# A hybrid decoder block on one core: 16x16 blocks gathered on chip, one solve for two mixers, sums of norms moved, no adds on POOL

## The chip, the core and the metric

The kernel runs on one core of a Trainium2 chip, and the metric is the device time of one execution in microseconds, as the median of several. A core has a matrix engine (TensorE, PE in the profile; PEld are its weight loads), a vector engine (VectorE, DVE), a scalar engine (ScalarE, ACT), a general one (GpSimd, POOL) and a fifth that here only issues transfers (SyncE, SP). Each engine runs its own queue in order. Sixteen DMA engines move data between DRAM and on-chip memory; a transfer is issued from the queue of SP, ACT or POOL.

## What is computed

One layer (`DEPTH = 1`) over 256 tokens of width 2048, in fp32:

```python
h = rms_norm(x, norm_mix_pre)
p = h @ w_in                                    # all mixers' inputs and gates
y_a = rglru_branch(...)                         # conv4, gated linear recurrence
y_b = gated_deltanet_branch(...)                # 8 heads of 128, chunks of 64
y_c = rwkv7_branch(...)                         # 16 heads of 64
m = sum_b sigmoid(gate_b) * (y_b @ w_branch[b])
x = x + rms_norm(m @ w_out, norm_mix_post)
h = rms_norm(x, norm_ffn_pre)
x = x + rms_norm((silu(h @ w_gate) * (h @ w_up)) @ w_down, norm_ffn_post)
```

Of the delta-rule mixer y_b the kernel needs, per head and chunk, the inverse of a unit lower triangular matrix:

```python
m = where(strict, beta[..., None] * (k @ k.T) * decay, 0)
sol = triangular_solve(m + eye(64), rhs, lower=True, unit_diagonal=True)
```

The RWKV mixer y_c is written as a recurrence over tokens in the reference; the kernel runs it by chunks of 64 and needs inverses of the same kind.

## The kernel before

**The products.** Every large product is done in three: activations and weights are each split in a high and a low part (`xh`, `xl`, `wh`, `wl`). `weights` (L190 on) loads 1 MB of weights into a tile `raw` from SP's queue (L203), ACT casts half of it into `wh` (L214), DVE subtracts to get `wl` (L216). There are three buffers each of `raw`, `wh` and `wl`. One `wh`/`wl` pair feeds 24 products of 256 columns (`block_b`, L241 to L243, the projections into the mixers) or 12 of 512 columns (`block_a`, L262 to L264, the rest).

**The mixers** run in four quarters `q` (two DeltaNet heads, four RWKV heads, a quarter of the LRU's channels). `rwkv_quarter` and `gdn_pair` are generators: each runs up to the `yield` in `inverse64`, then `lru_quarter` is written out, then the two are resumed, RWKV first. A scheduler lays each engine's queue out before the run, by the order in the program, dependences and its own estimate of durations; `high_priority` pulls an instruction ahead and `issue_after` sets a lower bound. So the mixers' small steps stand among the products of the next projections in PE's queue.

**The inverse** (`inverse64`, L370). A 64x64 triangle is inverted from its 16x16 diagonal blocks upwards. Lane p of DVE shall hold one row of each inverse and needs a whole block for it. RWKV has eight 64x64 matrices per lane half (`nu = 8`, out of `st`), DeltaNet four (`nu = 4`, out of `U`). Eight small DMAs from POOL's queue write a mixer's blocks to a DRAM tile `dblk` (L381), and one more reads it back into `B`, every block spread to 16 lanes (L383): 1 MB for RWKV, 512 KB for DeltaNet. Behind the `yield` come a copy of 16 unit columns (L388) and 15 steps of a product and a subtraction (L392, L393), for each mixer alone, held back behind `last`, the LRU's last instruction. Then merges to 32x32 and 64x64 follow, with transposes on DVE (L406, L417) and small products on PE.

**Norms and the end.** `product_a` (L1082) forms m @ w_out, and later the last product w_down, in four column blocks j and two halves t of 128 tokens. For each, ACT sums squares (L1090) and DVE multiplies with the norm's weight (L1091). After the last block the four sums are added (L1105, L1167), DVE and POOL form the reciprocal root (L296, L297), and the residual is added: L1110 behind w_out, whose result is then split for the next products (L308 to L313), and behind w_down, for each half, three blocks in one DVE instruction each (L1173), the fourth as a scaling on ACT (L1175) and an add on POOL (L1176). L1177 writes the output.

Of the kernel before, what the change touches and what calls it, by code (L numbers as in the profile page):

```python
# [8 lines left out]
F32 = mybir.dt.float32  # L9
F32R = mybir.dt.float32r  # L10
AF = mybir.ActivationFunctionType
# [129 lines left out]
class Builder:  # L141
# [227 lines left out]
    def inverse64(self, nu, diag16, block, transposed):  # L369
# [3 lines left out]
        nc, mp, n = self.nc, self.mp, nu * 32  # L373


        dd = self.dp.tile([8, nu, 16, 16], F32, name=self.uid("dblk"))
        for r in range(8):
            src = diag16(r)
            dst = dd[r].rearrange("(u n) j t -> j u n t", n=src.shape[2]) if len(src.shape) == 4 else \
                dd[r].rearrange("u j t -> j u t")  # L380
            nc.gpsimd.dma_start(dst, src)  # L381
        B = (self.u8 if nu == 8 else self.u4)("B").rearrange("p (u j t) -> p u j t", u=nu, j=16)
        nc.gpsimd.dma_start(B.rearrange("p u j t -> p (u j t)"),  # L383
                            dd.rearrange("r u j t -> r (u j t)").unsqueeze(1).to_broadcast([8, 16, nu * 256]))
        after = yield
        xc = mp.tile([P, nu, 16], F32, name=self.uid("xc"), tag=f"xc{nu}", bufs=1)
        with self.tc.issue_after(after):
            nc.vector.tensor_copy(xc, self.cst("d16", 0, 16).unsqueeze(1).to_broadcast([P, nu, 16]))  # L388
        for j in range(15):
            m = 15 - j  # L390
            t = mp.tile([P, nu, 16], F32, name=self.uid("xt"), tag=f"xt{nu}", bufs=2)
            nc.vector.tensor_tensor(t[:, :, 0:m], B[:, :, j, j + 1:16], xc[:, :, j:j + 1].to_broadcast([P, nu, m]), ALU.mult)  # L392
            nc.vector.tensor_tensor(xc[:, :, j + 1:16], xc[:, :, j + 1:16], t[:, :, 0:m], ALU.subtract)  # L393
# [63 lines left out]
    def rwkv_quarter(self, q, kS, rS, vS, up, y):  # L457
# [110 lines left out]
        X, = yield from self.inverse64(8, lambda r: st8[16 * r:16 * r + 16, :, (r < 4)::2, 16 * r:16 * r + 16],  # L568
# [128 lines left out]
    def gdn_pair(self, q_, qS, kS, vS, sz, y):  # L697
# [70 lines left out]
        J, JT = yield from self.inverse64(4, lambda r: h4(U)[16 * r:16 * r + 16, :, 16 * r:16 * r + 16],  # L768
# [61 lines left out]
    def lru_quarter(self, q, xS, gg, lru, y):  # L830
# [36 lines left out]
        last = nc.vector.tensor_tensor(h, h, gg, ALU.mult).ins  # L867
        nc.sync.dma_start(y[:, q * 512:(q + 1) * 512], h)
        return last


def build(tc, aps, out):
# [117 lines left out]
    def lru(q):  # L990
        s = direct(BLK_LX + q, 3)
        g = kept(BLK_LG + q, AF.Gelu_apprx_tanh)
        b.tmp_tag = "tl"
        return b.lru_quarter(q, s, b.get(g, "gg"), aps["lru"], y[0])

    for q in range(4):
        s = [direct(o + q, 1) for o in (BLK_RK, BLK_R, BLK_RV)]
        b.tmp_tag = "tr"
        rwkv = b.rwkv_quarter(q, *s, aps["up"], y[2])
# [4 lines left out]
        gdn = b.gdn_pair(q, *s, b.get(z, "z"), y[1])  # L1004
        next(gdn)
        last = lru(q)
        for tag, part in (("tr", rwkv), ("tg", gdn)):
            b.tmp_tag = tag
            with contextlib.suppress(StopIteration):
                part.send(last)  # L1010
# [71 lines left out]
    def product_a(w, ah, al, kts, hm, nw, ssq):  # L1082
        for j in range(4):
# [14 lines left out]
    product_a(aps["w_out"], mh, ml, KD, hm, n2, ssq)  # L1098
    x1d = [b.dp.tile([P, D], F32, name=f"x1d{t}") for t in range(2)]
    xh, xl = acts("h")  # L1100
    with tc.high_priority(FIRST):
        tots = [fp.tile([P, 6], F32, name=f"tot{t}") for t in range(2)]
        r1 = []
        for t in range(2):
            nc.vector.tensor_reduce(tots[t][:, 0:1], ssq[:, t], AX.X, ALU.add)  # L1105
            r1.append(b.rstd(fp, tots[t][:, 0:1], 1, 1.0 / D, EPS))
# [93 lines left out]
```

## Time and profile before

| | us |
|---|---|
| median of 3 runs | 1867.28 |
| their range | 1865.79 to 1868.06 |
| the profiled execution | 1864.51 |
| its span, first to last instruction | 1862.7 |
| PE busy | 1831.9 |
| DVE busy | 1113.6 |
| ACT busy | 850.6 |
| POOL busy | 82.5 |

The profile has one execution. Its times count from the first instruction; a group's line gives what it wrote and read (out<-in), its shape, how often it occurs, its busy time and the mean of one. The four mixer quarters lie between about 50 and 880 us, the branches and w_out up to 1111 us, the feed-forward part after that.

### The profile page before, as it was taken

What the parts mean: (1) busy time and instruction counts of PE and PEld (TensorE: products, weight loads), DVE (VectorE), ACT (ScalarE), POOL (GpSimd) and SP (SyncE); (2) the same over time, 40 slices, a digit from 0 to 9 for tenths busy, and PEclk for the clock granted to TensorE, in tenths of its full rate; (3) what the DMA queues carried; (4) which work ended last, traced back from release to release, by engine and by line L of the source; (5) the groups of instructions that cost most, each with busy time, mean ns of one, the idle gap of its engine ahead of it and who ended that gap; (6) DMA issues with size and microseconds to landing.
All of it is one profiled execution on the core that took longest, in us unless ns stands there. A gap on an engine that the chain in (4) does not pass through costs nothing.

```text
span 1862.7 us, 27857 instructions
## 1 busy us (share of the span) xinstructions
PE 1831.9 (98%) x11516; PEld 1582.6 (85%) x11516; DVE 1113.6 (60%) x1622; ACT 850.6 (46%) x1055; POOL 82.5 (4%) x150
## 2 busy tenths in 40 slices
PE   9999999999999999999999999999999999999997
PEld 9999997989898988778788878888888888888886
DVE  6768667766776576746665556554554445544444
ACT  7445345434543464444444446444444444443442
POOL 0011001200120002000000000000000000000000
PEclk9999999999999999999999999999999999999998
DMA  7565445653556345846865556555555555655553
GB/s 262 179 185 195 157 137 189 169 183 133 183 167 194 131 163 190 244 164 248 296 219 182 197 186 246 183 193 191 185 198 183 185 199 182 216 191 199 187 201 113
DMA packets 62799, 354.15 MB, mean 190 GB/s; under 512 B 9168, under 2 KB 10960, under 8 KB 23632
## 3 DMA queue, kind: packets, MB, share of 16 engines
q1 hardware_dynamic: 50832, 328.23, 50.9%
q10 hardware_dynamic: 7328, 15.36, 2.3%
q0 software_dynamic: 4512, 8.79, 1.9%
q8 instruction: 90, 1.47, 0.3%
q14 instruction: 37, 0.30, 0.0%
HBM read 337.27 MB, written 15.07 MB: 189 GB/s over the span
## 4 chain that ended last, share of the span: by engine, by line
PE 53%; issue 38%; DMA 3%; DVE 3%; ACT 1%; POOL 0%; ACTq 0%; DVEq 0%; SPq 0%; POOLq 0%
PE mm L264 8%; PE mm L263 8%; PE mm L262 8%; PE mm L242 7%; PE mm L243 7%; PE mm L241 7%; DMA raw<-in_w_in_dram 2%; DVE wl L216 1%; DMA raw<-in_w_mix_dram 1%; PE px L562 1%; PE pr L585 1%; PE pr L596 0%; ACT wh L214 0%; PE psa L592 0%; PE px L746 0%
## 5 line engine op out<-in xcount | busy, mean ns | idle before, releaser
L216 DVE TENSOR_TENSOR wl<-raw,wh 128x1024 fp32r<-128x1024 f32 x590 | 720.7, 1223 | 611.8 <-ACT wh L214 609.6
L214 ACT CAST wh<-raw 128x1024 fp32r<-128x1024 f32 x590 | 620.0, 1052 | 855.3 <-PE mm L264 592.3
L241 PE MATMUL mm<-xh,wh 128*128 128x256 f32 x1200 | 343.3, 286 | 5.0 <-ACT wh L214 5.0
L243 PE MATMUL mm<-xh,wl 128*128 128x256 f32 x1200 | 344.0, 287 | 2.5 <-DVE wl L216 1.5
L242 PE MATMUL mm<-xl,wh 128*128 128x256 f32 x1200 | 344.1, 287 | 1.6 <-DVE xl L909 1.5
L263 PE MATMUL mm<-wl,hh 128*128 128x512 f32 x704 | 274.7, 390 | 0.0
L264 PE MATMUL mm<-wh,hl 128*128 128x512 f32 x704 | 274.6, 390 | 0.0
L262 PE MATMUL mm<-wh,hh 128*128 128x512 f32 x704 | 251.0, 392 | 2.0 <-DVE rstd L296 1.5
L241 PEld LDWEIGHTS mm<-xh,wh 128*128 128x128 f32 x1200 | 231.1, 193 | 7.1 <-ACT wh L214 5.8
L243 PEld LDWEIGHTS mm<-xh,wl 128*128 128x128 f32 x1200 | 231.0, 193 | 4.2 <-DVE wl L216 1.9
L242 PEld LDWEIGHTS mm<-xl,wh 128*128 128x128 f32 x1200 | 231.1, 193 | 3.1 <-DVE xl L909 2.2
L262 PEld LDWEIGHTS mm<-wh,hh 128*128 128x128 f32 x704 | 132.4, 188 | 29.4 <-ACT hh L311 2.5
L263 PEld LDWEIGHTS mm<-wl,hh 128*128 128x128 f32 x704 | 132.6, 188 | 27.6 <-DVE wl L216 0.4
L264 PEld LDWEIGHTS mm<-wh,hl 128*128 128x128 f32 x704 | 132.5, 188 | 27.6
L263 PE MATMUL mm<-wl,xh 128*128 128x512 f32 x384 | 151.1, 394 | 0.9 <-DVE wl L216 0.9
L264 PE MATMUL mm<-wh,xl 128*128 128x512 f32 x384 | 150.5, 392 | 0.0
L262 PE MATMUL mm<-wh,xh 128*128 128x512 f32 x384 | 141.7, 393 | 0.5 <-ACT wh L214 0.5
L264 PE MATMUL mm<-wh,al 128*128 128x512 f32 x352 | 136.9, 389 | 0.0
L263 PE MATMUL mm<-wl,ah 128*128 128x512 f32 x352 | 136.9, 389 | 0.0
L262 PE MATMUL mm<-wh,ah 128*128 128x512 f32 x352 | 123.6, 389 | 0.0
L297 POOL TENSOR_TENSOR rstd<-rstd,mhalf 128x8 f32<-128x8 f32 (+3 forms) x23 | 29.7, 1296 | 1439.1 <-DVE rstd L296 1439.1
L263 PEld LDWEIGHTS mm<-wl,xh 128*128 128x128 f32 x384 | 72.1, 188 | 17.3 <-DVE wl L216 1.9
(294 smaller groups left out, 2009.0 us busy)
## 6 DMA issues: line engine op xcount, KB each, us to landing
raw<-in_w_in_dram SPq DMA_DIRECT2D x72, 1024.0 KB, 4.9
raw<-in_w_mix_dram SPq DMA_DIRECT2D x48, 1024.0 KB, 5.0
raw<-in_w_gate_dram SPq DMA_DIRECT2D x44, 1024.0 KB, 4.9
raw<-in_w_up_dram SPq DMA_DIRECT2D x44, 1024.0 KB, 4.9
raw<-in_w_down_dram SPq DMA_DIRECT2D x44, 1024.0 KB, 4.9
raw<-in_w_branch_dram SPq DMA_DIRECT2D x24, 1024.0 KB, 5.0
raw<-in_w_out_dram SPq DMA_DIRECT2D x16, 1024.0 KB, 4.8
keep<-stage ACTq DMA_DIRECT2D x28, 256.0 KB, 5.2
```

What stands on the lines that cost most here:

```text
L214: nc.scalar.copy(wh[:, :n], s)
L216: nc.vector.tensor_tensor(wl[:, :n], s, wh[:, :n].bitcast(F32), ALU.subtract)
L241: nc.tensor.matmul(o, hs, xh[:, k], start=(k == 0 and c == 0), stop=False, skip_group_check=True)
L242: nc.tensor.matmul(o, hs, xl[:, k], start=False, stop=False, skip_group_check=True)
L243: nc.tensor.matmul(o, ls, xh[:, k], start=False, stop=(k == kts - 1), skip_group_check=True)
L262: nc.tensor.matmul(ps[t], xh[:, k, ts], h, start=(k == 0), stop=False)
L263: nc.tensor.matmul(ps[t], xh[:, k, ts], l, start=False, stop=False)
L264: return nc.tensor.matmul(ps[t], xl[:, k, ts], h, start=False, stop=(k == kts - 1))
L297: nc.gpsimd.tensor_tensor(r, r, self.mhalf.to_broadcast([P, n]), ALU.pow)
L562: nc.tensor.matmul(ps[h][:, n * P:(n + 1) * P], bkc[hs, c, n], arc[hs, c, n], start=True, stop=True)
L585: nc.tensor.matmul(pq[bb, us], st[u][:, n, bb], sav[:, n, us], start=not n, stop=True, skip_group_check=True)
```

## The change

1. The 16x16 blocks no longer go through DRAM. `inverse64` copies them on chip into a tile `C` of 16 columns per matrix: for each group of 32 lanes, ACT writes one 16-column half times a 0/1 column (L398), DVE adds the other half times its 0/1 column (L396). Two blocks then lie under each other in 32 lanes.
2. A new `solve16` does the 15 steps for both mixers at once (12 matrices side by side). In step j a `stream_shuffle` on DVE (L378) spreads row j of both blocks over their 16 lanes each, into one of three row buffers; product (L379) and subtraction (L380) follow. `C`, the result and the three buffers share one tile `sv`, allocated ahead of `st` from the same pair of large buffers that `st` and `B` used.
3. The solve is written ahead of `lru_quarter`, and nothing holds it behind `last` any more.
4. In `product_a` the sums' addition and the reciprocal root of half t are written as soon as its last squares are summed, ahead of that half's last product with the norm's weight, for both norms.
5. At the end two of four blocks are scaled on ACT and added by DVE; POOL adds nothing.

```diff
-    def inverse64(self, nu, diag16, block, transposed):
...
-            nc.gpsimd.dma_start(dst, src)
...
-        after = yield
...
+    def solve16(self, C, xc, rows):
+        nc = self.nc
+        nu = C.shape[1]
+        nc.vector.tensor_copy(xc, self.cst("d16", 0, 16).unsqueeze(1).to_broadcast([P, nu, 16]))
         for j in range(15):
             m = 15 - j
...
+            t = rows[j % 3][:, :, 0:m]
+            nc.vector.stream_shuffle(t, C[:, :, j + 1:16], [j] * 16 + [16 + j] * 16)
+            nc.vector.tensor_tensor(t, t, xc[:, :, j:j + 1].to_broadcast([P, nu, m]), ALU.mult)
+            nc.vector.tensor_tensor(xc[:, :, j + 1:16], xc[:, :, j + 1:16], t, ALU.subtract)
+
+    def inverse64(self, C, diag, block, transposed):
...
+        for i in range(4):
+            for h in range(2):
+                s = diag(i, h)
+                c = C[32 * i:32 * i + 32]
+                c = c.rearrange("p (u n) t -> p u n t", n=s.shape[2]) if len(s.shape) == 4 else c
+                half = self.cst("blk16", 16 * h, 1)[32 * i:32 * i + 32]
+                if h:
+                    nc.vector.scalar_tensor_tensor(c, s, half, c, ALU.mult, ALU.add)
+                else:
+                    nc.scalar.activation(c, s, AF.Copy, scale=half)
+        xc = yield
...
+        sv = b.u8("sv")[:, 0:5 * 192].rearrange("p (i u t) -> p i u t", i=5, t=16)
+        C, xc = sv[:, 0], sv[:, 1]
...
-        last = lru(q)
...
+        b.solve16(C, xc, [sv[:, i] for i in range(2, 5)])
+        lru(q)
...
                     nc.scalar.activation(junk, ps[t], AF.Square, accum_out=ssq[:, t, j:j + 1])
+                    if j == 3:
+                        rms(t)
                     nc.vector.tensor_tensor(hm[:, t, js], ps[t], nw[:, js], ALU.mult)
...
+        for j in (3, 2):
+            nc.scalar.activation(o[j], o[j], AF.Identity, scale=r4[t])
+        for j in (0, 1, 3, 2):
+            if j < 2:
+                nc.vector.scalar_tensor_tensor(o[j], o[j], r4[t], x[j], ALU.mult, ALU.add)
             else:
-                nc.scalar.activation(od[:, t, js], od[:, t, js], AF.Identity, scale=r4[t])
-                nc.gpsimd.tensor_tensor(od[:, t, js], od[:, t, js], x1[t][:, js], ALU.add)
...
+                nc.vector.tensor_tensor(o[j], o[j], x[j], ALU.add)
```

How the queues stand. First POOL's, before, from the small DMAs of quarter 1 on (`slab` are the projections' outputs, whose margins POOL clears; `sav` is an RWKV tile):

```order
L542 MEMSET sav_2689 64x2x256 x2
L381 DMA dblk_3330<-U_3303 16x4x16 x8
L381 DMA dblk_2737<-st_2712 16x8x16 x8
L383 DMA B_3339<-dblk_3330 128x1x1024
L383 DMA B_2746<-dblk_2737 128x1x2048
L297 TENSOR_TENSOR rstd_4096<-rstd_4096,mhalf 128x4
```

Now the same place on POOL:

```order
L297 TENSOR_TENSOR rstd_2608<-rstd_2608,mhalf 128x8
L548 MEMSET sav_2637 64x2x256 x2
L297 TENSOR_TENSOR rstd_3990<-rstd_3990,mhalf 128x4
L336 MEMSET slab_688_5419 128x2x3
L336 MEMSET slab_902_6873 128x2x3
```

The eighteen DMAs between the clearing of `sav` and the next root are gone from the queue.

DVE in quarter 1, before, from the LRU's last product `h` on (`xc` is the solve's result, `xt` its product, `wl` a weight cast):

```order
L867 TENSOR_TENSOR h_3619<-h_3619,gg_3583 128x512
L388 COPY xc_3623<-cst_t 128x128
L388 COPY xc_3913<-cst_t 128x64
L341 TENSOR_TENSOR slab_632_4517<-mm_4519,rbc_294 128x2x256
L216 TENSOR_TENSOR wl_4701<-raw_4698,wh_4700 128x1024
L392 TENSOR_TENSOR xt_3915<-B_3339,xc_3913 128x4x15
L393 TENSOR_TENSOR xc_3913<-xc_3913,xt_3915 128x4x15
L392 TENSOR_TENSOR xt_3918<-B_3339,xc_3913 128x4x14
L393 TENSOR_TENSOR xc_3913<-xc_3913,xt_3918 128x4x14
L392 TENSOR_TENSOR xt_3921<-B_3339,xc_3913 128x4x13
L393 TENSOR_TENSOR xc_3913<-xc_3913,xt_3921 128x4x13
L216 TENSOR_TENSOR wl_4729<-raw_4698,wh_4728 128x1024
```

Now DVE in quarter 1, from the solve's first shuffle on (`ri`, `rec` and `h` are the LRU's):

```order
L378 STREAM_SHUFFLE sv_2561<-sv_2561 128x12x15
L378 STREAM_SHUFFLE sv_2561<-sv_2561 128x12x14
L378 STREAM_SHUFFLE sv_2561<-sv_2561 128x12x13
L216 TENSOR_TENSOR wl_4503<-raw_4472,wh_4502 128x1024
L869 TENSOR_TENSOR ri_3587<-ri_3587,ri_3593 128x512
L870 TENSOR_SCALAR rec_3599<-rec_3599 128x512
L379 TENSOR_TENSOR sv_2561<-sv_2561 128x12x15
L216 TENSOR_TENSOR wl_4537<-raw_4534,wh_4536 128x1024
L871 MEMSET rec_3599 128x2
L380 TENSOR_TENSOR sv_2561<-sv_2561 128x12x15
L216 TENSOR_TENSOR wl_4565<-raw_4534,wh_4564 128x1024
L873 SCALAR_TENSOR_TENSOR h_3607<-rec_3599,ri_3587 128x512
```

The solve now begins among the LRU's steps, three casts ahead of its `h`, and is spread over ten casts.

DVE at the end, for the second half of the tokens, before (`od` is the last product, `x1r` the residual):

```order
L1091 TENSOR_TENSOR od<-mm_15721,n_14570 128x512
L1167 TENSOR_REDUCE tot_16107<-ssq_14573 128x1
L296 TENSOR_SCALAR rstd_16109<-tot_16107 128x1
L1173 SCALAR_TENSOR_TENSOR od<-od,rstd_16109,x1r_14568 128x512 x3
L1196 UNCONDITIONAL_BRANCH
```

And now:

```order
L1180 TENSOR_REDUCE tot_15894<-ssq_14361 128x1
L1103 TENSOR_TENSOR od<-mm_15509,n_14358 128x512
L296 TENSOR_SCALAR rstd_15896<-tot_15894 128x1
L1191 SCALAR_TENSOR_TENSOR od<-od,rstd_15896,x1r_14356 128x512 x2
L1193 TENSOR_TENSOR od<-od,x1r_14356 128x512 x2
L1213 UNCONDITIONAL_BRANCH
```

The sum has moved ahead of the product with the norm's weight; the first step of the root has not.

## Rows read from the trace of the kernel before

**Rows 1.** The page's busy time by engine (us, share, instructions).

```profile
PE 1831.9 (98%) x11516; PEld 1582.6 (85%) x11516; DVE 1113.6 (60%) x1622; ACT 850.6 (46%) x1055; POOL 82.5 (4%) x150
```

**Rows 2.** Stretches: us, busy time (count) of each engine, granted clock, DMA share, GB/s.

```profile
182.00:203.00 21.00, 21.00 (x178) 21.00 (x177) 18.73 (x76) 8.13 (x8) 0.00 (x0) 1.00 0.54 188
350.00:370.00 20.00, 20.00 (x168) 20.00 (x168) 17.07 (x27) 7.26 (x8) 3.32 (x7) 1.00 0.83 171
370.00:385.00 15.00, 11.51 (x81) 11.10 (x81) 8.99 (x33) 4.09 (x4) 0.00 (x0) 0.89 0.84 247
...
560.00:580.00 20.00, 16.95 (x127) 16.54 (x126) 13.80 (x50) 5.52 (x6) 0.00 (x0) 0.91 0.80 226
740.00:760.00 20.00, 20.00 (x89) 16.53 (x89) 14.02 (x17) 11.66 (x15) 5.39 (x10) 1.00 0.75 178
755.00:780.00 25.00, 23.59 (x101) 18.44 (x100) 18.15 (x70) 10.54 (x11) 0.00 (x0) 1.00 0.88 270
```

**Rows 3.** Who waited for whom: us in total, times, longest us.

```profile
PE mm L241 <- ACT wh L214: 5.0, 2, 2.7
...
ACT wh L214 <- DMA raw<-in_w_in_dram: 30.3, 6, 8.9
...
ACT wh L214 <- DMA raw<-in_w_mix_dram: 9.8, 2, 5.1
```

**Rows 4.** Timeline, ACT, quarter 1: start, us, instruction, idle time before and its releaser.

```profile
375.56 1.99 ACT L214 CAST wh<-raw 128x1024 fp32r<-128x1024 f32 x2 [8.81 <-DMA raw<-in_w_in_dram]
```

**Rows 5.** DMA issues in 340 to 382 us: count, KB each, median us to landing.

```profile
raw<-in_w_in_dram SPq DMA_DIRECT2D x5, 1024.0 KB, 13.3
B<-dblk POOLq DMA_DIRECT2D x1, 1024.0 KB, 24.4
B<-dblk POOLq DMA_DIRECT2D x1, 512.0 KB, 7.7
```

**Rows 6.** DMA issues in 105 to 150 us (quarter 0).

```profile
raw<-in_w_in_dram SPq DMA_DIRECT2D x8, 1024.0 KB, 5.2
B<-dblk POOLq DMA_DIRECT2D x1, 1024.0 KB, 16.6
```

**Rows 7.** DVE groups by shape: busy us, mean ns of one, idle before.

```profile
L216 DVE TENSOR_TENSOR wl<-raw,wh 128x1024 fp32r<-128x1024 f32 x590 | 720.7, 1223 | 611.8 <-ACT wh L214 609.6 <-PE mm L243 0.5
...
L750 DVE SCALAR_TENSOR_TENSOR U<-px,btT,dm 128x128 f32<-128x128 f32 x16 | 4.8, 340 | 0.1
...
L406 DVE STREAM_TRANSPOSE DT<-D 128x256 f32<-128x256 f32 x4 | 1.8, 440 | 0.0
...
L392 DVE TENSOR_TENSOR xt<-B,xc 128x96 f32<-128x96 f32 x4 | 1.0, 253 | 0.0
```

**Rows 8.** Timeline, DVE, behind the last products of w_out.

```profile
1108.13 0.16 DVE L1105 TENSOR_REDUCE tot<-ssq 128x1 f32<-128x4 f32 x1 [2.49 <-ACT junk L1090]
1108.20 0.68 DVE L1091 TENSOR_TENSOR hm<-mm,n 128x512 f32<-128x512 f32 x1
...
1109.83 2.74 DVE L1110 SCALAR_TENSOR_TENSOR x<-hm,rstd,x 128x512 f32<-128x512 f32 x4 [0.89 <-POOL rstd L297]
1112.49 0.68 DVE L1091 TENSOR_TENSOR hm<-mm,n 128x512 f32<-128x512 f32 x1
...
1113.27 0.15 DVE L296 TENSOR_SCALAR rstd<-tot 128x1 f32<-128x1 f32 x1
```

**Rows 9.** Timelines at the end, second half of the tokens: DVE, ACT, POOL.

```profile
1851.69 0.68 DVE L1091 TENSOR_TENSOR od<-mm,n 128x512 f32<-128x512 f32 x1
...
1852.47 0.15 DVE L296 TENSOR_SCALAR rstd<-tot 128x1 f32<-128x1 f32 x1
1853.28 3.08 DVE L1173 SCALAR_TENSOR_TENSOR od<-od,rstd,x1r 128x512 f32<-128x512 f32 x3 [0.66 <-POOL rstd L297]
...
1851.29 0.19 ACT L1090 ACTIVATION_READ_ACCUMULATOR junk<-mm 128x1 f32 x1
...
1854.08 1.74 POOL L1176 TENSOR_TENSOR od<-od,x1r 128x512 f32<-128x512 f32 x1 [0.83 <-ACT od L1175]
```

More of the change, by code (lines that the diff above doesn't have):

```diff
@@ L866, in lru_quarter @@
         nc.vector.tensor_tensor_scan(h, rec, r, 0.0, ALU.mult, ALU.add)
-        last = nc.vector.tensor_tensor(h, h, gg, ALU.mult).ins
+        nc.vector.tensor_tensor(h, h, gg, ALU.mult)
         nc.sync.dma_start(y[:, q * 512:(q + 1) * 512], h)
-        return last
 def build(tc, aps, out):
@@ L993, in lru @@
         b.tmp_tag = "tl"
-        return b.lru_quarter(q, s, b.get(g, "gg"), aps["lru"], y[0])
+        b.lru_quarter(q, s, b.get(g, "gg"), aps["lru"], y[0])
     for q in range(4):
@@ L1003, in build @@
         b.tmp_tag = "tg"
-        gdn = b.gdn_pair(q, *s, b.get(z, "z"), y[1])
+        gdn = b.gdn_pair(q, *s, b.get(z, "z"), y[1], C[:, 8:12])
         next(gdn)
-        last = lru(q)
-        for tag, part in (("tr", rwkv), ("tg", gdn)):
+        b.solve16(C, xc, [sv[:, i] for i in range(2, 5)])
+        lru(q)
+        for tag, part, x in (("tr", rwkv, xc[:, 0:8]), ("tg", gdn, xc[:, 8:12])):
             b.tmp_tag = tag
             with contextlib.suppress(StopIteration):
-                part.send(last)
+                part.send(x)
         fill(FILL[q])
@@ L1097, in build, with rms1 @@
     ssq = fp.tile([P, 2, 4], F32, name="ssq")
-    product_a(aps["w_out"], mh, ml, KD, hm, n2, ssq)
+    tots = [fp.tile([P, 6], F32, name=f"tot{t}") for t in range(2)]
+    r1 = []
+    def rms1(t):
+        nc.vector.tensor_reduce(tots[t][:, 0:1], ssq[:, t], AX.X, ALU.add)
+        r1.append(b.rstd(fp, tots[t][:, 0:1], 1, 1.0 / D, EPS))
+    product_a(aps["w_out"], mh, ml, KD, hm, n2, ssq, rms1)
     x1d = [b.dp.tile([P, D], F32, name=f"x1d{t}") for t in range(2)]
@@ L1101, in build @@
     with tc.high_priority(FIRST):
[L1102 to L1106, printed above, removed]
         def group(t, k0):
@@ L1162, in build, with rms4 @@
     ssq = ap_.tile([P, 2, 4], F32, name="ssq2")
-    product_a(aps["w_down"], ah, al, KF, od, n4, ssq)
     r4 = []
-    for t in range(2):
+    def rms4(t):
         tot = ap_.tile([P, 1], F32, name=f"tot4{t}")
@@ L1168, in build @@
         r4.append(b.rstd(ap_, tot, 1, 1.0 / D, EPS))
+    product_a(aps["w_down"], ah, al, KF, od, n4, ssq, rms4)
     for t in range(2):
[L1170 to L1177 removed]
+        o = [od[:, t, j * 512:(j + 1) * 512] for j in range(4)]
+        x = [x1[t][:, j * 512:(j + 1) * 512] for j in range(4)]
+        for j in (3, 2):
[3 more added lines that the diff above has]
+                nc.vector.scalar_tensor_tensor(o[j], o[j], r4[t], x[j], ALU.mult, ALU.add)
+            else:
+                nc.vector.tensor_tensor(o[j], o[j], x[j], ALU.add)
+            (nc.sync, nc.scalar)[j % 2].dma_start(out[t * P:(t + 1) * P, j * 512:(j + 1) * 512], o[j])
     while b.cp:
```

35 lines of the change are left out of this document (9 added, 26 removed).

## The prediction

> **What bounds the kernel now.** I first read the page's busy time. TensorE (PE) is busy 1831.9 of 1862.7 us, 98% [rows 1], so a change can pay only by removing PE's idle time, lost rate, or the tail behind its last product. The diff keeps all 10351 matmuls. DVE and ACT have room over the whole span, so work taken from them is worth nothing in itself.
>
> Next the table by stretches, to find where PE runs below its rate. In 350 to 370 us it starts 168 products of 256 columns in 20 us, 0.119 us each. In 370 to 385 us it starts 81 where 126 would fit, at a mean granted clock of 0.89. In 560 to 580 us it starts 127 where 168 would fit, clock 0.91. [...] In 740 to 760 us it starts 89 of the 512-column kind in 20 us, 0.225 each; in 755 to 780 us 101 where 111 would fit [rows 2].
>
> Then ACT's waits, to see who is late. The high half of the weights, `wh`, waits for a weight load `raw` 30.3 us in six waits and 9.8 us in two [rows 3]. All eight lie in those three stretches; the longest ends at 375.56 [rows 4].
>
> Last the DMA issues. Around the first stall, in 340 to 382 us, a 1 MB weight load lands after 13.3 us (median) and the 1 MB spread `B<-dblk` after 24.4, with the other mixer's 512 KB one in the same stretch [rows 5]. In quarter 0 the larger spread stands alone in 105 to 150 us, and the weight loads around it land in 5.2 us [rows 6]; PE loses nothing in 182 to 203 us, the solve of that quarter [rows 2]. So I read the three stalls as DMA engines shared between the spreads and the weights: their share is 0.83 and 0.84 in 350 to 385 us against 0.54 in 182 to 203 [rows 2].
>
> **The change part by part.** *The DRAM round trip* (four times 16 small DMAs and two spreads, all on POOL's queue) goes. What it returns is the loss above. Quarter 1: (126 - 81) x 0.119 = 5.4 us. Quarter 2: (168 - 127) x 0.119 = 4.9. Quarter 3: (111 - 101) x 0.225 = 2.3. Sum 12.6 us. What is late next? Two loads start before the stall and would land in about 5 us, some 8 us earlier than now, while of the longest wait on ACT, 8.8 us [rows 4], only 2.7 us reached PE as idle time [rows 3]. So nothing of DMA remains on the path there; the bounds are 0 (the cause is another, see the rivals) and 12.6.
>
> *The gather.* Eight ACT copies and eight DVE multiply-adds of 32 lanes per quarter. Nearest row: a DVE multiply-add of 128x128 takes 0.34 us [rows 7], and these have 128 elements per lane or fewer: at most 2.7 us per engine and quarter. ACT is busy 7.26 of 20 us in 350 to 370 [rows 2] and mostly waits for PE to free a buffer, so they hide there; on path 0, at worst 0.5 us per quarter where DVE waits for an ACT copy with a cast queued behind it.
>
> *The solve.* Before: 60 small DVE operations per quarter. After: 30 of 1.5 times the mean length and 15 shuffles. With 12 blocks and 1 to 15 columns the mean is 96 elements, and a 128x96 product takes 0.253 us [rows 7]: 30 x 0.253 = 7.6 us. The trace has no shuffle. The nearest row moves data between lanes too, the stream transpose at 0.44 us for 256 elements; the bounds are 0.25 (as a product of 96) and 0.44, and I take 0.27, since the fixed part of both rows is alike. 15 x 0.27 = 4.1 us, 11.7 in all. The cover is what DVE has left: 24 products per `wl` cast take 24 x 0.119 = 2.86 us on PE, the cast 1.22 on DVE [rows 7], so 1.64 us are free per cast. In quarter 1 ten casts stand between the first shuffle and the last subtraction: 16.4 us for 11.7 us of solve and seven other operations, mostly 128x512 at 0.68 (about 4.8 us, an estimate). It just fits, as it did before (18.73 of 21 us in 182 to 203, PE never idle [rows 2]). On path 0.
>
> [...]
>
> *The handoff after w_out.* The code puts the sum and rstd ahead of the last product with n2. The order shows less: the sum moves ahead, but the product still stands between it and the rstd step. For the second half the product and rstd start at 1112.49 and 1113.27, with the sum between them. With the sum first, the product follows 0.07 later (as 1108.13 and 1108.20 show) and rstd 0.60 behind that (its 0.68 less the overlap), at 1113.16: 0.1 us [rows 8].
>
> *The tail.* Here everything is on the path. Now: the squares' sum is read at 1851.29 + 0.19 = 1851.48, but DVE is held by the first half until 1851.69; rstd starts at 1852.47 and the three multiply-adds at 1853.28; they end at 1856.36 [rows 9]. Three take 3.08 us here, where four of the same form and size take 2.74 at the handoff [rows 8]; what differs is POOL's add of 1.74 us beside them. After: the first half has two multiply-adds and two adds, 2.6 us in place of 3.1, so DVE is free by 1851.2; the sum starts at 1851.5, the product 0.07 and rstd 0.60 later, 1852.2. The step from there to the first multiply-add stays 0.81 (1852.47 to 1853.28): 1853.0. Then two multiply-adds of 0.67 (four in 2.74, so 0.67 from start to start [rows 8]), an add of 0.60 and a last of 0.68: 1855.6. The gain is 0.7 us. The second ACT scaling ends near 1854.4 by the pace of the first and is not last. If POOL were not the cause and the pace stayed at 1.03, it would be 1853.0 + 2.06 + 1.28 = 1856.3, and nothing gained.
>
> Sum: 12.6 + 0.1 + 0.7 = 13.4 us off. The profiled execution took 1864.51 (span 1862.7), 2.8 under the median of the three runs, 1867.28. I put the sum against the median: **1853.9**, say 1854.
>
> **The rivals.**
>
> *A new, smaller wait takes the place.* PE runs in order, and products of the mixers stand in its queue behind the solve's last transposes; where DVE is later than the planner thought, PE waits. For it: the solve just fits its casts, and an ACT copy of the gather now waits for DVE with casts behind it. Against: in 182 to 203 us DVE was as full and PE lost nothing. 0.5 to 2 us per quarter, 2 to 8 in all: 1856 to 1862, most likely 1859.
>
> *The shuffle is dear, and DVE becomes the bound: slower.* Place: the `wl` casts of every solve. Free time is 16.4 - 7.6 - 4.8 = 4.0 us plus two casts in hand (three buffers), 2 x 2.86 = 5.7: 9.7 us for 15 shuffles, so PE waits from 0.65 us per shuffle. The gain of 13.4 is eaten at 0.65 + 13.4 / 60 = 0.87 us; at 1.2 us, nearly three times the transpose row, the waits are 60 x 0.55 = 33 and the time 1853.9 + 33 = 1887. Against: the transpose at 0.44 with more than twice the elements.
>
> *The spreads are not what delays the weights: no change.* [...] For it: spreads land late in both kinds of quarter. Against: the DMA share of 0.83 and more, and the loads of `raw`, on SP's queue, slow to land in just that stretch. Then only the handoff and the tail pay: 1866.5. [...]
>
> **How the numbers follow.** The forecast, 1850 to 1857, has 0.70; the new wait 0.14 (0.01 of it beyond 1863.5); no change 0.08; slow by the shuffle 0.08. The low end, 1850, is the sum against the profiled execution itself (1851.1) less 1 for what a new order of PE's queue may save; the high end, 1862, takes in the new wait up to 2 us per quarter. Left out are no change and slow, 0.16, and the edges. 0.2%, about what a measurement here can tell, is 3.7 us: faster, below 1863.5, 0.83; same 0.09; slower 0.08.
>
> **What would show it.** Right: no ACT wait for `raw<-in_w_in` beyond a microsecond after 100 us, clock 1.00 in the mixers' part, 168 products per 20 us around each solve, POOL empty there; shuffles of 0.2 to 0.35 us; the last multiply-adds at 0.75; the span 13 us shorter. Wrong: PE idle behind `wl`, or behind the transposes (L412), in the solves; shuffles over 0.6 us; weight loads still landing in 10 us or more; the clock again at its low level there.

## The result, and the profile after

The changed kernel takes **1847.65 us** (median of four, 1846.92 to 1847.85) against 1866.53 (1865.38 to 1868.06) of the kernel before in the same comparison: ratio 0.9898, 95% interval 0.9883 to 0.9912. 1854 was forecast, within 1850 to 1862: the sign was right, the size too small by 6 us, and the time lies 2.4 us below the range. The traced execution took 1846.92.

The page's head and its busy times, which answer [rows 1]: PE is now busy 99% of a span 17.6 us shorter.

```profile
span 1845.1 us, 27756 instructions
PE 1827.5 (99%) x11516; PEld 1578.7 (86%) x11516; DVE 1123.7 (61%) x1652; ACT 863.8 (47%) x1089; POOL 41.0 (2%) x76
```

The table by stretches (from:to, length, busy time and instructions of PE, PEld, DVE, ACT, POOL, granted clock, DMA share, GB/s), for the stretches of [rows 2]:

```profile
182.00:203.00 21.00, 21.00 (x264) 20.83 (x263) 16.82 (x53) 7.33 (x7) 0.00 (x0) 1.00 0.53 185
350.00:370.00 20.00, 20.00 (x169) 20.00 (x168) 18.98 (x38) 8.55 (x9) 0.00 (x0) 1.00 0.54 187
370.00:385.00 15.00, 15.00 (x127) 15.00 (x126) 13.24 (x50) 5.25 (x5) 0.00 (x0) 1.00 0.54 190
560.00:580.00 20.00, 20.00 (x256) 19.83 (x255) 15.65 (x53) 7.34 (x7) 0.00 (x0) 1.00 0.50 177
740.00:760.00 20.00, 20.00 (x90) 16.54 (x89) 18.92 (x64) 9.16 (x10) 0.00 (x0) 1.00 0.84 285
755.00:780.00 25.00, 25.00 (x337) 20.27 (x336) 14.40 (x32) 10.84 (x14) 0.00 (x0) 1.00 0.58 194
```

PE starts 127 products where 81 stood in 370 to 385, the clock is at 1.00 and the DMA share at 0.54. In 740 to 760 the share is 0.84, as high as in the old stalls, and PE is never idle. Of ACT's waits for weight loads [rows 3], only the one at the start (and one of 0.2 us behind the mixers) is left:

```profile
ACT wh L214 <- DMA raw<-in_w_lo_dram: 2.3, 1, 2.3
```

The new instructions, by line (duration min/median/max in ns, first and last start):

```profile
L378 DVE LOAD_MASK_SELECT sv<-sv x60: 7/14/19, 163.6 to 756.7; - x60
L378 DVE STREAM_SHUFFLE sv<-sv x60: 202/264/399, 163.6 to 756.7; 128x180 f32<-128x180 f32 x4, 128x168 f32<-128x168 f32 x4, 128x156 f32<-128x156 f32 x4, 128x144 f32<-128x144 f32 x4
L379 DVE TENSOR_TENSOR sv<-sv x60: 172/254/341, 164.4 to 759.0; 128x180 f32<-128x180 f32 x4, 128x168 f32<-128x168 f32 x4, 128x156 f32<-128x156 f32 x4, 128x144 f32<-128x144 f32 x4
L398 ACT ACTIVATE sv<-st,cst_t x16: 384/397/402, 106.7 to 728.7; 32x128 f32<-32x128 f32 x16
L396 DVE SCALAR_TENSOR_TENSOR sv<-st,cst_t,sv x16: 337/342/352, 107.1 to 729.1; 32x128 f32<-32x128 f32 x16
```

The shuffle (L378) has a median of 0.264 us; 0.27 was taken.

Where the 17.6 us of span went: with the two traces aligned product by product, the lead of the changed kernel is -0.1 us at 360, 4.9 at 480 to 560, 10.8 at 650 to 680, 13.9 from 850 to 1090 and 14.2 behind w_out. So the three stalls were worth 5.0, 5.9 and 3.1 us. From the last product's start to DVE's last end it is 5.23 us, not 6.37: 1.1 more. And from there to the end of the span 4.06, not 6.38: 2.3 more, which no step of the prediction held.

### The profile page after: what moved, and what is told of

Read it like the earlier page. It is cut to its first block, busy times and chain, and to the rows that moved or that the text cites. A ratio compares the mean times of both kernels' runs of the same rounds, so it can differ in the third digit from the quotient of the medians.

```text
span 1845.1 us, 27756 instructions
## 1 busy us (share of the span) xinstructions
PE 1827.5 (99%) x11516; PEld 1578.7 (86%) x11516; DVE 1123.7 (61%) x1652; ACT 863.8 (47%) x1089; POOL 41.0 (2%) x76
## 3 DMA queue, kind: packets, MB, share of 16 engines
q8 instruction: 90, 1.47, 0.3%
## 4 chain that ended last, share of the span: by engine, by line
PE 96%; DVE 1%; ACT 1%; DMA 1%; issue 0%; POOL 0%; ACTq 0%; POOLq 0%; DVEq 0%; SPq 0%
PE mm L263 21%; PE mm L264 21%; PE mm L262 21%; PE mm L242 8%; PE mm L241 8%; PE mm L243 8%; PE tp L285 1%; PE px L568 1%; PE pr L603 1%; PE pr L592 1%; PE psa L599 1%; DMA raw<-in_w_branch_dram 1%; PE pst L609 0%; PE px L753 0%; PE px L482 0%
## 5 line engine op out<-in xcount | busy, mean ns | idle before, releaser
L262 PEld LDWEIGHTS mm<-wh,xh 128*128 128x128 f32 x384 | 72.1, 188 | 16.0 <-issue 1.3
```

The costliest lines, as they stand in the source:

```text
L262: nc.tensor.matmul(ps[t], xh[:, k, ts], h, start=(k == 0), stop=False)
```

## The experiments

Three dots in a diff stand for lines that are left out. Each result is given with its ratio to the kernel before, measured beside it, and the 95% interval.

### One part of the change at a time

**The solve alone**: the kernel before with the change's items 1 to 3, among them

```diff
...
-        last = lru(q)
...
+        b.solve16(C, xc, [sv[:, i] for i in range(2, 5)])
+        lru(q)
...
```

> The kernel before with the gather on chip, the shuffles and the common solve (the first three parts of the change); sums of the norms and the tail as before. Theory: the three stalls of quarters 1, 2 and 3 go and nothing takes their place, so the last product starts 13.9 us earlier (the two traces, aligned product by product, differ by 5.0, 5.9 and 3.0 us over the three quarters). Under theory A of the drain the time falls by 13.9 us, to 1852.6; under theory B the long drain goes as well, and it falls by 16.2 us, to 1850.3.

Measured: 1848.01 against 1867.04, ratio 0.9898 (0.9884 to 0.9911): **19.0 us, all of the gain** within what can be told. The long drain went too, 2.03 us in place of 7.91 with POOL's late add in both: theory B. Items 1 to 3 were not taken apart further: no run feeds the common solve from DRAM.

**The tail alone.**

```diff
...
-                nc.gpsimd.tensor_tensor(od[:, t, js], od[:, t, js], x1[t][:, js], ALU.add)
...
+                nc.vector.tensor_tensor(o[j], o[j], x[j], ALU.add)
...
```

> The kernel before with one part of the change: the output of the tail, in which two 512-column blocks of each half are scaled on ACT and added on DVE and POOL adds nothing. The mixers' solves, their DRAM round trip and the place of the norms' sums stay as before. In the trace of before, DVE's last operation ends 6.4 us ahead of the end of the span, in the changed kernel 4.1 us: POOL's last drain ran from 1854.04 to 1861.95, 2.5 us longer than SP's. Theory A: the drain is long because POOL's two late adds of 128x512 keep it busy. Then here the drain is below 1 us, SP ends the program, and the time falls by 2.3 (drain) + 1.1 (DVE's last operation earlier), 3.4 us, to about 1863.1 against 1866.5. Theory B: it is long because 74 transfers were issued on POOL's queue, which this kernel still has. Then POOL's drain is still 6 us or more here; it starts 3 us earlier, so the time falls by as much or less, 1 to 3.4 us, and the next run tells the two apart. Rival of the record: the adds are slow for another reason than POOL beside them, the pace of DVE's operations stays at 1.03 us, and the time falls by under 1 us.

Measured: 1862.43, ratio 0.9972 (0.9962 to 0.9983), 3 to 7 us off. DVE's last end comes 0.9 us earlier after the last product. POOL's last drain still takes 6.7 us (below): it begins earlier, since POOL has nothing to add, and so ends 0.3 us behind SP's instead of 2.5.

**The tail undone**, in the changed kernel.

```diff
...
-                nc.vector.tensor_tensor(o[j], o[j], x[j], ALU.add)
...
+                nc.gpsimd.tensor_tensor(od[:, t, js], od[:, t, js], x1[t][:, js], ALU.add)
...
```

> The changed kernel with the output of the tail as before: three multiply-adds on DVE, one ACT scaling and one POOL add per half. There are no transfers on POOL's queue but the two loads of x1. Theory A (POOL's late add makes the last drain long): the drain is again about 6 us beyond the add, and the time rises by 3.4 us, from 1847.6 to 1851.0. Theory B (the transfers on POOL's queue make it long): the drain is short, SP ends the program, and the time rises by what DVE and POOL lose alone, 1.1 us, to 1848.8.

Measured: 1848.32, ratio 0.9899 (0.9886 to 0.9913): 0.7 us slower than the changed kernel's median, theory B. So the tail is worth 3 us and more where the round trip stands, and under 1 where it is gone. The parts are not additive, since both shorten the same end. DVE's last three multiply-adds, beside POOL's add, take what they took before [rows 9]:

```profile
1839.86 3.08 DVE L1188 SCALAR_TENSOR_TENSOR od<-od,rstd,x1r 128x512 f32<-128x512 f32 x3 [0.66 <-POOL rstd L297]
```

Without the add two of them take 1.41 us, in the changed kernel and in the tail alone: 0.70 us each in place of 1.03.

**The sums of norms alone**, in the kernel before.

```diff
+                    if j == 3:
+                        rms(t)
                     nc.vector.tensor_tensor(hm[:, t, js], ps[t], nw[:, js], ALU.mult)
...
```

> The kernel before with only the sums of the norms written ahead of the last products with n2 and n4; solves and the tail's output as before. Theory: what stands between the sum and the rstd step stays, so only the sum leaves the path: 0.26 us at the handoff after w_out (0.1 was forecast) and 0.1 to 0.3 in the tail, 0.3 to 0.6 us in all, within what a measurement can tell, about 1866.1. Rival: the earlier Square of the last half seen in the changed kernel (0.42 us behind the last product's start instead of 0.81) comes from this part: then 0.4 us more.

Measured: 1864.92, ratio 0.9991 (0.9982 to 1.0). Its trace shows 0.24 us in the tail and, against the other traces, 0.26 at the handoff; the rest of the 2.1 us can't be told from the spread of its runs (1863.2 to 1867.6). Inconclusive beyond the 0.5.

### What POOL's last drain costs

The drains of the last line, by kernel (the longest of a row's three numbers is POOL's wait at the end): before, the changed kernel, the tail alone, and, from the runs told below, the small writes put back, the spreads put back, and both.

```profile
L1196 POOLq DRAIN  x3: 40/102/7913, 1854.0 to 1862.5; - x3
```
```profile
L1213 POOLq DRAIN  x3: 40/93/836, 1837.8 to 1844.8; - x3
```
```profile
L1198 POOLq DRAIN  x3: 40/93/6722, 1853.5 to 1860.8; - x3
```
```profile
L1224 POOLq DRAIN  x3: 40/93/6075, 1837.9 to 1844.9; - x3
```
```profile
L1233 POOLq DRAIN  x3: 40/102/1817, 1838.9 to 1845.9; - x3
```
```profile
L1239 POOLq DRAIN  x3: 40/93/7048, 1838.3 to 1845.9; - x3
```

Counted from the end of POOL's last operation, the drain takes 0.26 us with 2 transfers issued on POOL's queue in the whole program, 0.91 with 10, 1.24 with 14, 2.22 with 26, 3.53 with 42, 5.49 with 66, 6.14 with 74 and 6.47 with 78, with or without adds: 0.26 + 0.082 us for each further transfer, though the last of them (the loads of `x1`) was issued some 700 us before. It goes by their number and not their bytes (the 66 are nearly all of 4 and 8 KB, the 26 hold four times 2.7 MB). Before, 74 of them behind a late add made POOL end 2.5 us behind SP; with the 66 and no add, POOL ends ahead of SP and nothing is lost.

### The kernel before, traced again

> The kernel before, traced once more. Three kernels with its mixers gave their last product at 1849.99, 1851.31 and 1853.24, so the stalls behind the weights differ from execution to execution. The traced one of the record took 1864.51, 2 to 2.5 us under the median; I expect the last product of another one between 1850 and 1854, its three stalls between 14 and 17 us, and about 1867.

Measured: 1867.31 (eight runs, ratio 1.0003). The traced execution spans 1865.9; its last product starts at 1853.20, 3.2 us later than in the trace of the rows. Its waits for weights (total, times, longest):

```profile
ACT wh L214 <- DMA raw<-in_w_in_dram: 30.4, 6, 9.2
ACT wh L214 <- DMA raw<-in_w_mix_dram: 4.7, 1, 4.7
```

The first is as in [rows 3], the second half of it, but PE's loss up to 900 us, against the changed kernel, is 17.3 us and not 13.9. The granted clock differs. In the first trace it is 1.00 in 265 to 285 us, ahead of the first stall, and 0.91 in 560 to 580 [rows 2]; here, in the same work:

```profile
265.00:285.00 20.00, 20.00 (x145) 18.22 (x143) 10.99 (x19) 10.93 (x16) 3.27 (x2) 0.91 0.45 154
562.00:582.00 20.00, 16.81 (x118) 16.31 (x116) 13.50 (x45) 5.03 (x5) 0.00 (x0) 0.83 0.81 233
```

Of the 3.4 us, 1.6 are lost ahead of 360 us, and 2.1 in the stalls of quarters 1 and 2; quarter 3 loses 0.3 less. The trace that the prediction was read from was of a mild execution.

### What made the stalls

**The round trip put back, unused.** `free` is the unused part of the tile `sv`, `spare` a tile of its own, and `m` at most 1088.

```diff
...
+            nc.gpsimd.dma_start(dst, src)
+        flat = dd.rearrange("r u j t -> r (u j t)").unsqueeze(1).to_broadcast([8, 16, nu * 256])
...
+        nc.gpsimd.dma_start(self.free[:, 0:m], flat[:, :, 0:m])
+        if nu == 8:
+            nc.gpsimd.dma_start(self.spare, flat[:, :, m:m + 640])
...
```

> The changed kernel with the DRAM round trip put back beside it, its result read by nobody: per quarter the 16 small writes and the two spreads on POOL's queue, issued behind the same products as before (the larger spread moves 1728 of its 2048 columns, for want of space, 0.86 MB in place of 1 MB). The solve still runs on the gathered copy and waits for no transfer. Theory A, that of the record (the transfers of the round trip hold up the weight loads): PE stalls again on the weights in quarters 1, 2 and 3 and drops to the low clock there, 10 to 17 us in all, and the time is 1858 to 1865. Theory B (the stalls came from what waited for the spread: the solve's products and DVE operations placed behind its landing, with the casts behind them): no stall, and the time is 1848 to 1849, at most 0.3 us of it from a longer drain on POOL.

Measured: 1857.56, ratio 0.9957 (0.994 to 0.9974): 10 us. But ACT waits for no weight load in the mixers, and the planner had changed PE's order: 3762 of its 11516 products stand at another place in the trace. So the halves were run apart, both with the order of PE, DVE, ACT and SP unchanged: the first diff line alone, and the others with an input as their source,

```diff
...
+        flat = self.src[:, 0:nu * 256].unsqueeze(1).to_broadcast([8, 16, nu * 256])
...
```

> The changed kernel with the 16 small writes per quarter put back, unused, and no spread: half of what the run with the whole round trip put back (1857.6, last product 9.6 us later than in the changed kernel) holds. Theory A (the spreads' bytes hold up the weights and the instructions): the loss is gone or under 2 us, 1847.5 to 1849.5. Theory C (the writes, 64 and 32 bytes apiece, do it: in a short stretch they are most of the packets): most of the 9.6 us stays, 1854 to 1858. For the drain on POOL, 64 of the 72 transfers remain: if it goes with their number, it is again 6 us or more beyond the last power step.

Measured: 1848.01 (0.9886 to 0.9916 as ratio). Nothing.

> The changed kernel with the spreads alone, unused: the same bytes as in the run with the whole round trip, from an input in DRAM instead of the written blocks, behind a one-element copy on POOL that waits for the same products; no small writes. Theory A: most of the 9.6 us stays, 1854 to 1858. Theory C: it is gone, 1847.5 to 1849.5. The drain on POOL with some 14 transfers of its queue in all: near 1 us if it goes with their number.

Measured: 1847.99 (0.9885 to 0.9918). Nothing either. Then the same transfers as in the 10 us run, the spreads first and the writes behind them:

> The changed kernel with the same transfers as the run with the whole round trip put back unused (1857.6), on the same queue, in the other order: the spreads first, from an input in DRAM, and the 16 small writes behind them. In that run the writes held POOL's queue for 16 x 0.52 us, so that the larger spread was issued at 354.0, 1.3 us behind the first weight load after some 14 us without one, and the other at 364.0; with the spreads alone the first two were issued at 339.6 and 340.2, where the DMA engines have little to do, and nothing was lost. Theory T (it is the time at which the spread comes, on top of the weight loads): nothing is lost here either, 1847.5 to 1849.5. Theory B+C (the number of transfers or the bytes of writes and spreads together): the 10 us are back, 1856 to 1860. The drain on POOL is 6 us or more under both.

Measured: 1847.94 (0.9889 to 0.9918). So number and bytes alone are not what costs; but in both runs most of the spreads, issued from 340 us on, lay ahead of the next weight load (at 353 us). Two runs then put the spreads where the weight loads are, behind a copy on POOL into a one-element tile `go` that waits for the solve, and for the gather:

```diff
...
+                go = nc.gpsimd.tensor_copy(go, t[0:16, 0, 0:1]).ins
+                with self.tc.issue_after(go):
+                    self.spread()
...
```
```diff
...
+        go = nc.gpsimd.tensor_copy(go[96:112], C[96:112, 0, 0:1]).ins
+        with tc.issue_after(go):
+            b.spread()
...
```

> The changed kernel with the spreads alone, unused, from an input in DRAM, and late: on POOL's queue behind a one-element copy that waits for the first product of the solve, near 359 us in quarter 1, when the weight loads come every 4 to 6 us. The instructions of PE, DVE, ACT and SP stand in the same order as in the changed kernel; in the run with the whole round trip put back (10 us) the planner had also put 1583 of PE's 8898 products in another order. Theory T (the bytes cost when they fall on the weight loads): weight loads land in 8 us or more there, and PE loses 3 to 10 us, 1850.5 to 1857.5. Theory O (the loss there came from the other order, not from the transfers): 1847.5 to 1848.5.

> As the single late spreads (which cost nothing: 1847.6), but behind the last operation of the gather instead of the first product of the solve, so that the first two spreads are issued near 352.5 in quarter 1, 1 us ahead of the first weight load after 15 us without one, and not at 361, behind two that have landed. In the kernel before the spreads were issued at 352.1 and 353.8. The order of the other engines is that of the changed kernel. Theory R (the stalls of before come from spreads that lie on the refill of the weight buffers): the first loads land in 10 us instead of 5, ACT waits for weight loads 5 us or more per quarter, and PE loses 2 to 5 us in each of quarters 1 and 2: 1851 to 1857. Theory O (this order of instructions hides a single spread wherever it comes): 1847.5 to 1848.5.

Measured: 1847.61 and 1847.42 (ratios 0.9901 and 0.99). **Nothing lost, on top of the weight loads.** The second one's stretch, and the same stretch of the kernel before:

```profile
353.00:378.00 25.00, 25.00 (x211) 25.00 (x210) 23.24 (x67) 9.44 (x9) 2.24 (x4) 1.00 0.93 265
```
```profile
352.00:378.00 26.00, 22.51 (x186) 22.10 (x184) 17.18 (x32) 7.26 (x8) 1.32 (x3) 1.00 0.93 204
```

The DMA engines are busy 0.93 in both, yet they move 265 GB/s in one and 204 in the other. The loads behind the spreads land after 5.6, 10.5 and 11.1 us here, and PE does not wait for them; before, after 10.9, 18.3 and 18.0.

**The whole 1.5 MB at once**, at that place, to DRAM.

```diff
...
+        for n in (1024, 2048):
+            to = self.dp.tile([P, n], F32, name=self.uid("spare"))
+            self.nc.gpsimd.dma_start(to, flat[:, :, 0:n])
...
```

> As the spreads at the refill (which cost nothing: 1847.4, the first loads behind them landing in 5.6, 10.5 and 11.1 us), but whole and both at once as in the kernel before, 0.5 MB and 1 MB within 1 us, unused, written to DRAM for want of space in SBUF; the order of the other engines is unchanged. In the kernel before the loads of that stretch landed in 10.9, 18.3 and 18.0 us. Theory S (three raw buffers and three casts in hand absorb a load of some 11 us, not one of 18): loads take 14 us or more, ACT waits for them 3 us or more per quarter, and PE loses 2 to 5 us per quarter with the low clock behind it, 1853 to 1862. Theory O (this order hides any single spread): 1847.5 to 1848.5.

Measured: 1847.08 (0.9875 to 0.9908). The bytes pass at 316 GB/s in 353 to 368 and the loads land in 4.8, 9.6 and 7.9 us: theory S could not be tried at its 14 us, and no run of the changed kernel put 1.5 MB into SBUF, the on-chip memory, at once as the kernel before does. Taken in shorter stretches, though, the rates say more than the mean of 265 against 204. First the run at the refill, beside its first spreads and in the pause ahead of the last; then the kernel before beside its spreads; then this run, whose spreads go to DRAM:

```profile
358.00:364.00 6.00, 6.00 (x52) 6.00 (x52) 5.75 (x13) 2.09 (x2) 0.00 (x0) 1.00 1.03 199
364.00:368.00 4.00, 4.00 (x35) 4.00 (x35) 3.96 (x9) 1.05 (x1) 0.58 (x1) 1.00 0.99 406
```
```profile
354.00:376.00 22.00, 19.93 (x166) 19.72 (x165) 13.85 (x28) 5.22 (x6) 0.45 (x1) 1.00 1.00 215
```
```profile
358.00:364.00 6.00, 6.00 (x52) 6.00 (x51) 5.75 (x13) 2.10 (x2) 0.00 (x0) 1.00 1.03 356
```

Beside a spread into SBUF the busy DMA engines moved 199 and 215 GB/s in the two kernels, and the weights themselves ran slower: in the kernel before an 8 KB packet of them took 614 ns (median) in 352 to 378, and 309 in 390 to 402. What differs is how long it lasts: 22 us in one piece before, at the refill 6 us, a pause of 4 at 406 GB/s, and some 6 us more. That the long piece is what makes the loads 18 us late is argued from these rows; no run puts it back alone, and why the rate falls beside these spreads stays open.

**Twice the spreads, late.**

```diff
+        for _ in range(2):
+            self.nc.gpsimd.dma_start(self.free, flat[:, :, 0:1088])
+            self.nc.gpsimd.dma_start(self.spare, flat[:, :, 1088:1728])
+            self.nc.gpsimd.dma_start(self.free[:, 0:1024], flat[:, :, 0:1024])
```

> As the run before, each spread made twice over (2.7 MB per quarter instead of 1.4), the order of the other engines again unchanged. Theory T: the loss of the single late spreads at least doubles, since the slack of the weight loads (some 8 us per load in hand) is used up once. Theory O: 1847.5 to 1849.

Measured: 1857.56, ratio 0.995 (0.9933 to 0.9966): 10 us lost where 1.4 MB cost nothing. The weights are not what is late (1.9 us of waits on ACT). PE waits 6.6 us, in three quarters, in the middle of 96 products of 32x32, for nothing that the profile shows (the wait of one line, then the stretch around one of them, with the granted clock at 0.85):

```profile
PE px L433 <- issue: 6.6, 3, 2.5
```
```profile
395.00:400.00 5.00, 2.75 (x105) 2.44 (x104) 1.97 (x4) 0.00 (x0) 0.58 (x1) 0.85 0.87 312
```

The run with the round trip put back has the same wait (2.5 us, L435). In both, a 16 KB packet of the instruction queue starts within 0.3 us of the beginning of that wait (390.8 and 396.1), which ends some 2.3 us later. That PE's own instructions came late there, behind the spreads, is the author's guess from these times; no run shows it. Of the other two waits here one begins 0.1 us behind such a packet and one 1.1 us. And the kernel before has a wait of 1.0 us of this kind at 596, 1.3 us behind such a packet and without a spread beside it:

```profile
PE mm L243 <- issue: 1.0, 1, 1.0
```

**Half of the writes on SP's queue**, in the kernel before.

```diff
...
-            nc.gpsimd.dma_start(dst, src)
+            (nc.sync if nu == 8 else nc.gpsimd).dma_start(dst, src)
...
```

> The kernel before, its eight writes per quarter for the larger solve issued on SP's queue (0.33 us apiece) beside the other eight on POOL's (0.51 us), so that POOL's queue is free about 4 us earlier. Theory T: the larger spread is issued near 348 to 350 instead of 353.8 in quarter 1 and partly ahead of the weight loads, and the stalls shrink; by the part of the spread's landing time (24 us) that no longer lies on the weights, 2 to 6 us in all, 1860 to 1864. Theory B+C: the transfers and bytes are the same, and so is the time but for a drain on POOL that is shorter with 32 of its 72 transfers gone: 1864 to 1866. Rival: the writes hold SP's queue with the weight loads behind them, and it is slower than 1867.

Measured: 1878.96, ratio 1.0061 (1.0044 to 1.0077): slower, by another way than the rival said. Both spreads are still issued at 352, the weight loads beside them again land late (16.1, 15.1 and 13.0 us), and the planner now has DVE begin the solve ahead of the next casts (PE's order changed as well). DVE waits for the spreads with the casts behind it, and PE for the casts (DVE's wait in this run, then PE's two; before, DVE's wait is 1.1 us):

```profile
DVE xt L392 <- DMA B<-dblk: 34.3, 4, 12.4
```
```profile
PE mm L243 <- DVE wl L216: 10.7, 2, 7.6
PE mm L263 <- DVE wl L216: 9.6, 2, 9.3
```

### How much room DVE has

```diff
...
-            nc.vector.stream_shuffle(t, C[:, :, j + 1:16], [j] * 16 + [16 + j] * 16)
+            for _ in range(4):
+                nc.vector.stream_shuffle(t, C[:, :, j + 1:16], [j] * 16 + [16 + j] * 16)
...
```

> The changed kernel with each of the 60 shuffles made four times over (same result). A shuffle measures 0.264 us in the trace of the changed kernel, so each step then costs 1.06 us and DVE has 45 x 0.264 = 11.9 us more work per quarter. By the record's bound PE waits from 0.65 us per shuffle on: 15 x (1.06 - 0.65) = 6.1 us per quarter, 24 us in all, 1872. Rival: DVE's room is larger than the bound says, since more than ten casts can stand around the solve before PE needs its result; then the time stays within 2 us of 1847.6.

Measured: 1855.79 (two runs, 1854.05 and 1857.54), ratio 0.9943 (0.9923 to 0.9963): 8.3 us slower, a third of the 24 expected. But the load was smaller than the expectation says. Around 361 us a shuffle of 0.38 to 0.41 us begins 0.26 to 0.31 us behind the one ahead of it, and DVE's busy time rises by 28.9 us over the program (from 1123.7), not by 180 x 0.264 = 47.5:

```profile
PE 1828.0 (99%) x11516; PEld 1581.3 (85%) x11516; DVE 1152.6 (62%) x2012; ACT 864.9 (47%) x1090; POOL 42.9 (2%) x76
```

By that a step's shuffles cost 0.264 + 28.9 / 60 = 0.75 us, and the bound of 0.65 gives 60 x 0.10 = 6 us (an estimate). The planner, which knew of the shuffles, also put 4216 of PE's 11516 products at another place, so the run does not test the bound cleanly. DVE is then full in 755 to 780 (25.00 of 25):

```profile
755.00:780.00 25.00, 23.50 (x104) 19.10 (x103) 25.00 (x83) 11.46 (x12) 0.00 (x0) 1.00 0.65 211
```

### A faster version: the rstd step really first

`b.step` is the root's first step on DVE (L296).

```diff
...
-                    nc.vector.tensor_tensor(hm[:, t, js], ps[t], nw[:, js], ALU.mult)
+                    with tc.issue_after(b.step) if j == 3 else contextlib.nullcontext():
+                        nc.vector.tensor_tensor(hm[:, t, js], ps[t], nw[:, js], ALU.mult)
```

> The changed kernel with the rstd step really ahead of the last product with n2 and n4: the product is held behind it in DVE's queue (in the changed kernel the sum went ahead, and the product still stood between it and the rstd step). Theory: the rstd step starts 0.6 us earlier at both places, and the product runs beside POOL's power step of 0.54 us. The tail's multiply-adds start 0.45 to 0.55 us earlier, and so does the first transpose after w_out: 0.9 to 1.1 us off, 1846.6. Rival: at the handoff the first transpose waits for another thing (the product with n2 of the same half), then only the tail's 0.5 us comes, 1847.1.

Measured: 1846.46 beside 1847.46 of the changed kernel, and 1845.90 when measured again (ratio 0.9891, 0.9876 to 0.9906). DVE's timeline in the tail (start, duration), of the changed kernel and of this one:

```profile
1836.96 0.16 DVE L1180 TENSOR_REDUCE tot<-ssq 128x1 f32<-128x4 f32 x1
1837.04 0.68 DVE L1103 TENSOR_TENSOR od<-mm,n 128x512 f32<-128x512 f32 x1
1837.64 0.14 DVE L296 TENSOR_SCALAR rstd<-tot 128x1 f32<-128x1 f32 x1
1838.43 1.41 DVE L1191 SCALAR_TENSOR_TENSOR od<-od,rstd,x1r 128x512 f32<-128x512 f32 x2 [0.66 <-POOL rstd L297]
```
```profile
1836.29 0.16 DVE L1181 TENSOR_REDUCE tot<-ssq 128x1 f32<-128x4 f32 x1 [0.43 <-ACT junk L1100]
1836.47 0.15 DVE L296 TENSOR_SCALAR rstd<-tot 128x1 f32<-128x1 f32 x1
1836.55 0.68 DVE L1104 TENSOR_TENSOR od<-mm,n 128x512 f32<-128x512 f32 x1
1837.29 1.41 DVE L1192 SCALAR_TENSOR_TENSOR od<-od,rstd,x1r 128x512 f32<-128x512 f32 x2
```

From the sum to the first multiply-add it is 1.00 us in place of 1.47. It is the fastest of all kernels here, though by less than its interval separates from the changed kernel.

## Why the prediction was right and wrong

- **Right: where the time is.** The solve's part carries the gain, PE's stalls in quarters 1 to 3 go, nothing takes their place, and the granted clock stays at 1.00 in their stretches (before, behind quarter 1's wait, it was 0.50 in 378.5 to 381.5 us). (The 10351 matmuls that the prediction keeps stand in no row; the page counts 11516 on PE in both kernels.)
- **Right: the new work and its cover.** Gather: 4 x 0.397 + 4 x 0.345 = 3.0 us on ACT and 4 x 0.342 + 4 x 0.274 = 2.5 on DVE per quarter (2.7 each was the bound, so ACT's is just above it), with no wait of PE behind it. Shuffle 0.264 (0.27), product 0.254 (0.253); the shuffle took 4% more than the product. With the 60 shuffles the trace has 60 `LOAD_MASK_SELECT`, of 14 ns in the median, too little to count.
- **Wrong: the term of the round trip, 12.6 us.** The run of the solve alone gives 19.0. Three things are missing from the term. The windows cut off 1.3 us that the aligned traces show (13.9): the three quarters lost 5.0, 5.9 and 3.1 where 5.4, 4.9 and 2.3 were read, and the wait of 1.0 us at 596, for one, lay outside them. The execution that they were read from was 2.8 us below the median because it lost less to the stalls and the low clock (13.9 against 17.3 in another trace), and **the sum was put against the median** as if the loss of that one had stood in all; against the execution itself it was 1851.1, and that number was only used for the low end. Last, the 2.3 us of drain: the prediction took 72 transfers off POOL's queue and followed the tail to DVE's last multiply-add, but not the drain of that queue at the end (6.14 us with 74 transfers, 0.26 with 2).
- **Half shown: the cause.** That the loads of the weights land late behind the spreads, in packets that took twice as long (614 ns against 309), is what the rows show, and the gain came where they said. That a DMA share of 0.83 and more explains it is refuted: at 0.93, with the spreads on the weight loads, the changed kernel loses nothing, and it has 0.84 by itself in 740 to 760. In the rows it was the landing times (18 us, where 11 did no harm) that told, not the share. That the transfers alone made the stalls is not shown: put back in pieces into the order of the changed kernel, 1.4 MB per quarter cost nothing; the whole trip put back lost 10 us in another order of PE and without a wait for weights; and none of these runs had the old length of the overlap.
- **Not settled: the bound on DVE.** Waits were to start at 0.65 us per shuffle. Four shuffles per step cost DVE 0.75 us of busy time each step, for which the bound gives some 6 us, and 8.3 were measured, with another order on PE. The slow rival stayed away because a shuffle takes 0.264.
- **Small terms.** Handoff 0.26 in the trace (0.1 forecast); DVE's end in the tail 1.1 earlier (0.7 forecast), of which under 1 us arrives in the medians. That the multiply-adds are slow beside POOL's adds was read rightly: without them the two take 1.34 us from their start to the next instruction, 2 x 0.67 as forecast, and with them put back 1.03 each.
- **The rivals.** The new wait did not come. The rival of no change held that the spreads are not what delays the weights; a busy share of the DMA engines alone is no cause indeed (0.93 without a loss), but the delay of the loads did not stay (13.3 us to landing before, in 340 to 382, 5.0 in 340 to 395 now, medians).

## What to carry to other kernels

A loss read from one trace belongs to that execution (13.9 us here, 17.3 in another): subtract it from that one's time, and where stalls carry the sum, trace the kernel twice. Price a competing transfer by its neighbours' landing times against the slack of the buffers behind them, since a busy DMA share alone does not say that anyone waits (0.93 here, with nothing lost). Follow a removed transfer to the end of the program as well, where its queue is drained (2.3 us here). And before an experiment is read as a dose, look at how much of the dose the engine really took, and whether the queues kept their order.

## What the runs showed of the hardware

- Each transfer issued on POOL's queue added 0.082 us to POOL's last drain, from 2 (0.26 us) to 78 of them (6.47 us).
- DMA engines that were busy all the time (share 0.99 to 1.03) moved 199 and 215 GB/s beside spreads into SBUF, in two kernels, 406 in a pause between them, and 356 beside spreads to DRAM. An 8 KB packet of weights took 614 ns beside the spreads and 309 without.
- Doubling transfers from 1.4 to 2.7 MB per quarter cost 10 us in one step. In the trace PE waits 6.6 us within bursts of tiny products, and not for late weights.
- A multiply-add of 128x512 on DVE took 1.03 us beside an add on POOL and 0.70 without it.
- Shuffles in a row on DVE overlapped: 180 more, of 0.26 to 0.29 us in the median, raised its busy time by 28.9 us. In the changed kernel three of 0.37 to 0.39 us begin 0.26 and 0.27 us apart.
- Two executions of one kernel, with like waits of PE for weights (5.0 and 5.3 us), lost 13.9 and 17.3 us: the granted clock was lower in the second, 0.83 against 0.91 in quarter 2's stall.
